# Decoder block on one Trainium2 core: a fourth step by seven products in every second early block, low parts in two halves, and changed service of banks and first transposes

## The chip, the cores and the metric

The kernel runs on one core of one Trainium2 chip. A core has a matrix engine (TensorE, PE in the profile; its weight loads are shown as PEld), VectorE (DVE), ScalarE (ACT), GpSimd (POOL) and SyncE (SP), each with an instruction queue of its own that is worked through in order, and DMA queues that SP, ACT and POOL feed. Matrix products are accumulated in eight banks of PSUM; everything else lives in SBUF or in DRAM. The metric is the device time of one execution in microseconds, as the median of the runs shown.

## The reference

One layer of a hybrid decoder on 256 tokens of 2048 channels, in float32. A normalised input is multiplied by one wide matrix; its columns feed dilated window attention and a gated linear recurrence, the two results are mixed by per-channel gates, and a SwiGLU feed-forward stage follows.

```python
a = rmsnorm(h, norm_mix_pre[layer])
proj = a @ w_in[layer]
q_a, k_a, v_a, q_r, f_r, i_r, g_r, gate_a, gate_r = split_columns(proj)
...
y = jax.nn.sigmoid(gate_a) * (attn @ w_attn_branch[layer]) + jax.nn.sigmoid(gate_r) * (r_out @ w_hgrn_branch[layer])
h = h + rmsnorm(y @ w_mix_out[layer], norm_mix_post[layer])
a = rmsnorm(h, norm_ffn_pre[layer])
gt, up = jnp.split(a @ w_ffn_gate_up[layer], [D_FF], axis=-1)
ff = (jax.nn.silu(gt) * up) @ w_ffn_down[layer]
h = h + rmsnorm(ff, norm_ffn_post[layer])
```

`g_r` passes through silu and a gain, the gates through a sigmoid; the values and `i_r` are only scaled by the row's norm factor.

## The kernel before

**Products in parts.** Each float32 operand is split into a high part (a ScalarE copy to a rounded type) and a low part (VectorE: operand minus high part). One product of a 128-row tile is then three TensorE instructions: high by high, high by low, low by high. The weights stream through SBUF: SP loads a tile `raw` (three buffers), `split` makes the parts two steps ahead of their use (`AHEAD` = 2), `multiply` or `multiply_wide` issues the products.

**Order.** The order is written out by hand. The loop at line 1346 takes step n of all blocks and issues, in this order: the block's `pre` if it is its first step; the split of step n+2 and the load behind it (lines 1350 to 1352); the products of step n; a piece of the evacuation that is under way (`advance(evacs)`); a piece of each lane (`advance_lanes`: lane 0 holds the opening's norm and tables, lane 1 the sums `pair_sums`). What stands earlier in this order stands earlier in each engine's queue. Evacuations are generators; each `yield` ends a piece.

**Blocks.** The run begins with two narrow blocks for the two halves of `g_r` (COL_GR), eight steps each of 12 products and 1024 weight columns in all. During the first of them `transpose_in` also brings x in, two 128-column pieces at a time: four transposes on TensorE, two copies on ScalarE (line 498), two low parts on VectorE (line 502). Their evacuation is `evac_g`. Then come eight wide blocks, the **early blocks**, 0 to 7: gates, values and `i`, 1024 columns each, eight steps each of 256 rows. Their evacuation `evac_kept` adds, scales and writes the result to DRAM (`kept`); it is read back later by GpSimd's queue. After them come the forget and query columns of the recurrence, the query and key columns with attention worked in between, the branches, the mix, ten wide feed-forward blocks and two wide down blocks.

**Steps by seven.** A wide step covers two row tiles, two column halves and two token halves: eight products, 24 instructions (a plain step). Where the order marks it, the step is done by seven products of sums (Strassen's scheme), 21 instructions. For that VectorE and ScalarE form, in `split_wide`: sums of weights (lines 333, 339, 340), their high parts (338, 341), the high part of the differences' operand `dh` (344), the low part of the sums (345) and the low part `dl` (347). The sums of x for it come from `pair_sums` and are kept in `x7`. Four products of each block (p1, p6, p5, p7) have banks of their own. After the block's last seven step, `gather` (lines 392 to 396) copies p1 and makes four sums; after the block's last step, `evac_kept` adds the other four banks to them. The two sets of four banks swap from block to block (`flip`). In the early and feed-forward blocks three steps of eight are by seven; the order is `EIGHT`: the pairs are (row pair, by seven), so steps 2, 4 and 6 are by seven.

**Buffers.** High parts `w` and low parts `wl` have three buffers, so the parts of step n+2 can be written once step n-1's products are done. `sum`, `dh` and `dl` have one buffer each. All 512-wide evacuation tiles `e` share six.

The lines to follow are 36 to 38 (orders), 319 to 348 (`split_wide`), 388 to 397 (`gather`), 619 to 620 (masks), 642 to 648 (transposes and sums), 663 to 677 (`evac_kept`), 738 to 754 (`evac_g`), 1293 to 1299 (early blocks) and 1346 to 1377 (the loop).

Of the kernel before, what the change touches and what calls it, by code (L numbers as in the profile page):

```python
# [13 lines left out]
F32 = mybir.dt.float32  # L14
# [5 lines left out]
P = 128  # L20
# [12 lines left out]
COL_QR, COL_FR, COL_IR, COL_GR = 9216, 10240, 11264, 12288  # L33
COL_GA, COL_GB = 13312, 15360

X7 = H7 = (0, 1, 2)
EIGHT = [(3, 0), (4, 0), (0, 1), (5, 0), (1, 1), (6, 0), (2, 1), (7, 0)]
DOWN = [[(m, m in by7) for m in range(KF // 2)] for by7 in (range(4, 20, 3), range(3, 19, 3))]

# [50 lines left out]
def tile_hybrid_block(ctx: ExitStack, tc: tile.TileContext, t, out):  # L90
# [105 lines left out]
        return pool["now"].tile([P, 512], F32, tag="p", bufs=n, name=nm(s))  # L196

    cs = kp.tile([P, 2, S], F32, name="cs")
    amask = kp.tile([P, 2, 512], F32, name="amask")
    lmask = kp.tile([P, len(LEVELS), 64], F32, name="lmask")  # L200
    gainr = kp.tile([P, HW], F32, name="gainr")
    tabs = kp.tile([P, 4, S], F32, name="tabs")
    bounds = kp.tile([P, 64], F32, name="bounds")
    lb, lb1 = bounds[:, :8], bounds[:, 8:16]


    blocks, seq, units = [], [], []
# [111 lines left out]
    def split_wide(st):  # L319

        b, raw = st.block, st.raw
        m, by7 = b.order[st.i]
        prep = b.prep(m, by7) if b.prep else iter(())
        next(prep, None)
        hi, lo = wslot(), p3("wl", F32R, 2048, 3)
        if not by7:
            nc.scalar.activation(hi, raw, AF.Copy)  # L327
            next(prep, None)
            nc.vector.tensor_sub(lo, raw, hi.bitcast(F32))  # L329
            st.parts = hi, lo  # L330
            return
        s, d = p3("sum", F32, 2048, 1), raw[:, 512:]
        nc.vector.tensor_sub(  # L333
            s[:, :1024].rearrange("p (a c) -> p a c", a=2),
            raw[:, 512:1536].rearrange("p (a c) -> p a c", a=2),
            raw[:, None, :512].to_broadcast([P, 2, 512]),
        )
        nc.scalar.activation(hi[:, :1024], s[:, :1024], AF.Copy)  # L338
        nc.vector.tensor_add(s[:, 1024:1536], raw[:, 512:1024], s[:, 512:1024])
        nc.vector.tensor_sub(s[:, 1536:], raw[:, 1536:], s[:, 1024:1536])  # L340
        nc.scalar.activation(hi[:, 1024:], s[:, 1024:], AF.Copy)  # L341
        next(prep, None)
        dhi, dlo = p3("dh", F32R, 1536, 1), p3("dl", F32R, 1536, 1)
        nc.scalar.activation(dhi, d, AF.Copy)  # L344
        nc.vector.tensor_sub(lo, s, hi.bitcast(F32))  # L345
        next(prep, None)
        nc.vector.tensor_sub(dlo, d, dhi.bitcast(F32))  # L347
        st.parts = hi, lo, dhi, dlo
# [230 lines left out]
    def opening():  # L579
        ss, s2 = small("ss"), small("s2")  # L580
        yield from sumsq(ss, xt[:3])
        nc.scalar.dma_start(gainr, t["hgrn_norm_gain"].to_broadcast([P, HW]))
        nc.scalar.dma_start(rowg[0:16], t["norm_ffn_pre"][0].rearrange("(a p) -> a p", p=P))
        nc.scalar.dma_start(
            rowg[16:32], t["hgrn_lower_bounds"].rearrange("l (a p) -> (l a) p", p=P)
        )
        nc.scalar.dma_start(cs, t["rope"])
        yield from sumsq(ss, xt[3:], 3)
        add_parts(s2[:, :2], ss)
        rsqrt_mean(r1c, s2[:, :2], D)  # L590
# [12 lines left out]
        nc.tensor.transpose(ps[:, :32], rowg[:32], ident[:32, :32])  # L603
        yield
        nc.vector.tensor_copy(colg[:, 16:48], ps[:, :32])
        l0, l1 = colg[:, 32:40], colg[:, 40:48]
        m, e0, e1 = small("m"), small("e0"), small("e1")
        nc.vector.tensor_max(m, l0, l1)
        nc.vector.tensor_sub(e0, l0, m)
        nc.vector.tensor_sub(e1, l1, m)  # L610
        nc.scalar.activation(e0, e0, AF.Exp)
        nc.scalar.activation(e1, e1, AF.Exp)
        nc.vector.tensor_add(e1, e0, e1)
        nc.vector.reciprocal(e1, e1)
        nc.vector.tensor_mul(lb, e0, e1)
        nc.vector.tensor_scalar(lb1, lb, -1.0, 1.0, op0=OP.mult, op1=OP.add)
        ready.add("lb")
        yield
        nc.sync.dma_start(amask, t["amask"])
        nc.sync.dma_start(lmask, t["lmask"])  # L620

    def keep_warm(n):

# [38 lines left out]

    def evac_kept(key, fn):
        def go(b):
            dst = keep(key, 1024)
            for s, g in ((0, 0), (0, 1), (1, 0), (1, 1)):
                src = b.bank[s, g]
                if b.rest:
                    e = b.rest[s, g]
                    nc.vector.tensor_add(e, src, e)  # L670
                    src = e
                else:
                    e = eslot()
                nc.scalar.activation(e, src, fn, scale=r1c[:, s : s + 1])
                nc.scalar.dma_start(dst[:, s, g * 512 : (g + 1) * 512], e)
            yield
        return go

    def end_early():
        flush(evacs)  # L680
        enter("middle")
        attnT.append(Split("attnT", 8))
        recT.append(Split("recT", 8))
        for half in range(2):
            gN[half] = hslot("g")
            back(gN[half], ("g", half), 0, 512, True)
            iN[half] = hslot("v")
            back(iN[half], "i", 512 * half, 512 * half + 512, True)

    def values_back(half):  # L690

# [46 lines left out]
    def evac_g(half):  # L738
        def go(banks):
            while "r1c" not in ready:  # L740
                yield
            dst, there = hslot("g"), keep(("g", half), 512)
            for i in range(2):
                ps = banks[i]
                s = ptile("sig")
                nc.scalar.activation(s, ps, AF.Sigmoid, scale=r1c[:, i : i + 1])
                yield
                nc.vector.scalar_tensor_tensor(  # L748
                    out=s, in0=ps, scalar=r1c[:, i : i + 1], in1=s, op0=OP.mult, op1=OP.mult
                )  # L750
                nc.vector.tensor_mul(dst[:, i, :], s, gainr[:, half * 512 : (half + 1) * 512])
                nc.gpsimd.dma_start(there[:, i, :], dst[:, i, :])
                yield
        return go
# [33 lines left out]
    def attention(pair, hh):  # L788
# [4 lines left out]
        for par in range(2):  # L793
            own = slice(par * P, (par + 1) * P)
            ps = aux()
            for g in range(3):
# [6 lines left out]
            p = ptile("p")  # L803
            m = small("m")
            nc.vector.tensor_tensor_reduce(
                out=p, in0=ps, in1=amask[:, par, :], scale=1.0, scalar=3e38,
                op0=OP.add, op1=OP.min, accum_out=m[:, 0:1],
            )
            nc.scalar.activation(p, p, AF.Exp, scale=-1.0, bias=m[:, 0:1], accum_out=m[:, 1:2])
# [27 lines left out]
    def recurrence(half):  # L837
# [36 lines left out]
        def products(lev, w):  # L874

            ps = aux()
            if w < 64:
                for e in range(8):
# [5 lines left out]
                yield  # L884
                nc.vector.copy_predicated(
                    at.rearrange("p (e n w) -> p e n w", e=8, w=2 * w)[:, :, :, w:],
                    lmask[:, lev, :].rearrange("p (n w) -> p n w", w=w)[:, None, :, :]
                    .to_broadcast([P, 8, 64 // w, w]).bitcast(I32),
                    ps.rearrange("p (e n w) -> p e n w", e=8, w=w),
                )  # L890
# [403 lines left out]
             (COL_GA + 1024, ("a", 1), AF.Sigmoid), (COL_GB + 1024, ("r", 1), AF.Sigmoid)]  # L1294
    early += [(COL_V + 1024 * g, ("v", g), AF.Copy) for g in range(3)] + [(COL_IR, "i", AF.Copy)]
    for n, (col, key, fn) in enumerate(early):
        add_seven(w_in, (col, col + 512), EIGHT, xT, lambda m: x7[m],
                  evac_kept(key, fn), flip=n % 2 == 1, turn=1,
                  pre=(lambda: flush(lanes[1])) if n == 0 else None)
    for half in range(2):  # L1300
        add_wide(w_in, KD, COL_FR + 512 * half, xT, evac_f(half))
        if half == 0:
# [27 lines left out]
    for j in range(2):  # L1330
        add_seven(t["w_ffn_down"][0], (1024 * j, 1024 * j + 512), DOWN[j], act,
                  lambda m: a7[m], evac_down, prep=prep_act, flip=j == 1,
                  pre=begin_down if j == 0 else None, turn=3 if j == 0 else None)

    load_x(0, 0, 256)
    load(0, 0)
    load_x(0, 256, 512)
# [8 lines left out]
    for n, st in enumerate(seq):  # L1346
        b, i = st.block, st.i
        if i == 0 and b.pre:
            b.pre()
        if n + AHEAD < len(seq):  # L1350
            split(seq[n + AHEAD])
            load_behind(seq[n + AHEAD])
        if n >= len(seq) - 3:
            continue
        if type(b) is Wide:
            multiply_wide(st)
            if i == b.last7:
                gather(b)
        else:
            multiply(st)  # L1360
            if b.post:
                b.post(i)
        advance(evacs)
        if turns and type(turns[0]) is not list:
            advance(turns)
        advance_lanes()
        if type(b) is not Wide:
            if st.last:
                evacs.append(b.evac(b.banks))
            continue  # L1370
        if i == b.turn:
            flush(evacs)
            if turns:
                turn_act(turns.popleft(), b)
        if st.last:
            evacs.append(b.evac(b))
            advance(evacs)
# [63 lines left out]
```

## Time and profile before

| | |
|---|---|
| runs | 1718.56, 1719.61, 1720.99 us |
| median | 1719.61 us |
| profiled execution, whole time | 1718.82 us |
| profiled execution, span from first to last instruction | 1717.0 us |
| granted TensorE clock | 0.999 |
| busy: TensorE, VectorE, ScalarE, GpSimd | 1700.6, 1373.6, 900.3, 21.7 us |
| eight early blocks | about 58 to 394 us |

A timeline row gives start in us, length in us, engine, line, operation, result and sources, sizes, and, in square brackets, how long the engine was idle before it and what ended the idle time. A row that stands for several instructions ends in their count. The lines of a group give count, busy time, mean length in ns and idle time before. Lengths of TensorE's instructions overlap (each is shown as some 0.39 us), so time on TensorE is best read from starts.

### The profile page before, as it was taken

The page shows a single profiled execution, that of the slowest core. Times are in us where ns is not written, and L with a number is a line of the kernel's source. Part 1 is how long each engine was busy: PE and PEld are TensorE (multiplying, and loading weights), DVE is VectorE, ACT ScalarE, POOL GpSimd, SP SyncE. Part 2 cuts the span into 40 slices and gives each one's busy share as a digit, 9 for nine tenths or more (in the row PEclk, how much of TensorE's full clock was granted, in tenths as well). Part 3 has the DMA queues.
Part 4 walks back from the last instruction along what each step waited for, and adds up shares of the span by engine and source line. Part 5 has one row for each costly group of instructions (what it writes and reads, how often), then busy time and mean ns, then how long its engine had stood idle before and what let it go on. Part 6 is the DMA issues. An engine that isn't in the chain of part 4 may idle for free.

```text
span 1717.0 us, 21554 instructions
## 1 busy us (share of the span) xinstructions
PE 1700.6 (99%) x8347; PEld 1428.2 (83%) x8347; DVE 1373.6 (80%) x1497; ACT 900.3 (52%) x1014; POOL 21.7 (1%) x38
## 2 busy tenths in 40 slices
PE   9999999999999999999999999999999999999997
PEld 6788888888888898888888878888888888888886
DVE  6888888885677887877666578888888888898998
ACT  6555555554435434544444466555555555665663
POOL 0000000000000000000000000000000000000000
PEclk9999999999999999999999999999999999999999
DMA  7666666667544645565456745555555555666653
GB/s 264 234 242 231 228 221 220 226 234 244 191 148 160 221 160 172 179 202 168 163 173 201 246 165 196 197 198 200 201 201 202 201 202 197 219 197 214 202 197 115
DMA packets 208741, 344.77 MB, mean 201 GB/s; under 512 B 10960, under 2 KB 77696, under 8 KB 208640
## 3 DMA queue, kind: packets, MB, share of 16 engines
q1 hardware_dynamic: 198496, 318.61, 55.0%
q10 hardware_dynamic: 7232, 14.31, 2.3%
q0 software_dynamic: 2912, 10.49, 1.8%
q8 instruction: 65, 1.06, 0.3%
q14 instruction: 36, 0.29, 0.0%
HBM read 331.83 MB, written 11.53 MB: 200 GB/s over the span
## 4 chain that ended last, share of the span: by engine, by line
PE 94%; DVE 3%; ACT 1%; DMA 1%; issue 1%; SPq 0%; ACTq 0%; DVEq 0%
PE acc L131 62%; PE aux L131 31%; DVE w L293 1%; DMA raw<-in_w_in 0%; PE aux L818 0%; DMA gpost<-in_norm_mix_post 0%; PE aux L491 0%; PE acc L1132 0%; DVE fz L1261 0%; PE aux L1132 0%; ACT w L327 0%; PE aux L479 0%; ACT junk L1215 0%; ACT w L292 0%; DVE sig L748 0%
## 5 line engine op out<-in xcount | busy, mean ns | idle before, releaser
L293 DVE TENSOR_TENSOR w<-raw,w 128x1024 fp32r<-128x1024 f32 (+1 forms) x225 | 274.2, 1219 | 189.4 <-ACT w L292 188.8
L292 ACT ACTIVATE w<-raw 128x1024 fp32r<-128x1024 f32 (+1 forms) x225 | 236.9, 1054 | 294.1 <-PE acc L131 248.3
L131 PE MATMUL acc<-xT,w 128*128 128x256 f32 (+1 forms) x2048 | 370.4, 339 | 0.0
L131 PEld LDWEIGHTS acc<-xT,w 128*128 128x128 f32 x2048 | 311.6, 188 | 43.3
L329 DVE TENSOR_TENSOR wl<-raw,w 128x2048 fp32r<-128x2048 f32 x122 | 279.0, 2286 | 41.6 <-ACT w L327 41.5
L327 ACT ACTIVATE w<-raw 128x2048 fp32r<-128x2048 f32 x122 | 232.9, 1909 | 110.1 <-PE aux L131 43.9
L345 DVE TENSOR_TENSOR wl<-sum,w 128x2048 fp32r<-128x2048 f32 x66 | 151.2, 2291 | 68.9 <-ACT w L341 68.8
L131 PE MATMUL acc<-w,hT 128*128 128x512 f32 x622 | 181.5, 391 | 0.3 <-ACT hT L498 0.3
L338 ACT ACTIVATE w<-sum 128x1024 fp32r<-128x1024 f32 x66 | 70.2, 1063 | 188.4 <-DVE sum L333 176.7
L131 PE MATMUL acc<-w,xT 128*128 128x512 f32 x536 | 155.8, 392 | 2.2 <-ACT xT L498 1.6
L131 PEld LDWEIGHTS acc<-w,hT 128*128 128x128 f32 x622 | 116.0, 188 | 24.7 <-ACT hT L498 0.5
L131 PE MATMUL aux<-w,hT 128*128 128x512 f32 x430 | 135.6, 389 | 0.0
L131 PEld LDWEIGHTS acc<-w,xT 128*128 128x128 f32 x536 | 99.7, 188 | 24.2 <-ACT xT L498 1.9
L347 DVE TENSOR_TENSOR dl<-raw,dh 128x1536 fp32r<-128x1536 f32 x66 | 115.6, 1751 | 0.0
L131 PE MATMUL aux<-w,xT 128*128 128x512 f32 x344 | 108.5, 389 | 0.0
L344 ACT ACTIVATE dh<-raw 128x1536 fp32r<-128x1536 f32 x66 | 97.3, 1474 | 0.0
L131 PEld LDWEIGHTS aux<-w,hT 128*128 128x128 f32 x430 | 80.7, 188 | 16.8
L131 PE MATMUL acc<-w,yT 128*128 128x512 f32 x384 | 88.2, 390 | 0.1
L131 PEld LDWEIGHTS acc<-w,yT 128*128 128x128 f32 x384 | 71.8, 188 | 15.3 <-DVE w L293 0.6
L131 PE MATMUL acc<-w,a 128*128 128x512 f32 x268 | 83.7, 389 | 0.0
L131 PE MATMUL aux<-wl,hT 128*128 128x512 f32 x215 | 83.6, 389 | 0.0
L131 PE MATMUL acc<-wl,hT 128*128 128x512 f32 x215 | 83.6, 389 | 0.0
(257 smaller groups left out, 2669.7 us busy)
## 6 DMA issues: line engine op xcount, KB each, us to landing
raw<-in_w_in SPq DMA_DIRECT2D x271, 512.0 KB, 4.6
raw<-in_w_ffn_gate_up SPq DMA_DIRECT2D x176, 512.0 KB, 4.4
raw<-in_w_ffn_down SPq DMA_DIRECT2D x88, 512.0 KB, 4.8
raw<-in_w_mix_out SPq DMA_DIRECT2D x32, 512.0 KB, 4.9
kept<-e ACTq DMA_DIRECT2D x32, 256.0 KB, 4.3
raw<-in_w_hgrn_branch SPq DMA_DIRECT2D x16, 512.0 KB, 4.5
raw<-in_w_attn_branch SPq DMA_DIRECT2D x16, 512.0 KB, 4.4
v<-kept POOLq DMA_DIRECT2D x8, 512.0 KB, 7.1
```

The lines of the kernel that those rows point to most:

```text
L131: nc.tensor.matmul(ps, lhsT, rhs, start=start, stop=stop, skip_group_check=True)
L292: nc.scalar.activation(wh[:, k], raw[:, k], AF.Copy)
L293: nc.vector.tensor_sub(wl[:, k], raw[:, k], wh[:, k].bitcast(F32))
L327: nc.scalar.activation(hi, raw, AF.Copy)
L329: nc.vector.tensor_sub(lo, raw, hi.bitcast(F32))
L338: nc.scalar.activation(hi[:, :1024], s[:, :1024], AF.Copy)
L344: nc.scalar.activation(dhi, d, AF.Copy)
L345: nc.vector.tensor_sub(lo, s, hi.bitcast(F32))
L347: nc.vector.tensor_sub(dlo, d, dhi.bitcast(F32))
```

## The change

- `X7` has four members, so a fourth pair of x's tiles gets its sums. A second order `FOUR` has steps 1, 3, 5 and 6 by seven; odd early blocks use it, even ones keep `EIGHT`.
- `dh` and `dl` have two buffers in the early stage.
- In early and feed-forward blocks the low part of the sums is made in two halves of 1024. In the down blocks (`b.prep`) it stays whole.
- The masks `amask` and `lmask` are allocated in the middle stage and loaded by GpSimd's queue at its beginning, no longer by SP's queue in the opening.
- `evac_kept` does its four bank additions first, then the four activations, two in each piece; the writes to DRAM go by GpSimd's queue, no longer by ScalarE's.
- `evac_g` reads the banks on ScalarE alone: a sigmoid and a scaled copy for each side, all in the first piece; VectorE multiplies afterwards, from SBUF.
- The second g block's first evacuation piece is issued at the start of early block 0, where lane 1 was flushed before; lane 1 is flushed at the start of block 1.
- In the first two steps of the run, the split of step n+2 and the load behind it are issued after the step's products and transposes.

```diff
-X7 = H7 = (0, 1, 2)
+X7, H7 = (0, 1, 2, 3), (0, 1, 2)
+FOUR = [(4, 0), (0, 1), (5, 0), (1, 1), (6, 0), (2, 1), (3, 1), (7, 0)]
 EIGHT = [(3, 0), (4, 0), (0, 1), (5, 0), (1, 1), (6, 0), (2, 1), (7, 0)]
...
-    amask = kp.tile([P, 2, 512], F32, name="amask")
-    lmask = kp.tile([P, len(LEVELS), 64], F32, name="lmask")
...
+    masks = {}
...
         next(prep, None)
-        dhi, dlo = p3("dh", F32R, 1536, 1), p3("dl", F32R, 1536, 1)
+        dhi, dlo = (p3(x, F32R, 1536, 2 if pool["name"] == "early" else 1) for x in ("dh", "dl"))
         nc.scalar.activation(dhi, d, AF.Copy)
-        nc.vector.tensor_sub(lo, s, hi.bitcast(F32))
+        for x in (slice(0, 2048),) if b.prep else (slice(0, 1024), slice(1024, 2048)):
+            nc.vector.tensor_sub(lo[:, x], s[:, x], hi[:, x].bitcast(F32))
         next(prep, None)
         nc.vector.tensor_sub(dlo, d, dhi.bitcast(F32))
...
-        yield
-        nc.sync.dma_start(amask, t["amask"])
-        nc.sync.dma_start(lmask, t["lmask"])
...
     def evac_kept(key, fn):
         def go(b):
-            dst = keep(key, 1024)
-            for s, g in ((0, 0), (0, 1), (1, 0), (1, 1)):
-                src = b.bank[s, g]
-                if b.rest:
-                    e = b.rest[s, g]
-                    nc.vector.tensor_add(e, src, e)
-                    src = e
-                else:
-                    e = eslot()
-                nc.scalar.activation(e, src, fn, scale=r1c[:, s : s + 1])
-                nc.scalar.dma_start(dst[:, s, g * 512 : (g + 1) * 512], e)
+            dst, at = keep(key, 1024), [(0, 0), (0, 1), (1, 0), (1, 1)]
+            for k in at:
+                nc.vector.tensor_add(b.rest[k], b.bank[k], b.rest[k])
+            for s, g in at:
+                e = b.rest[s, g]
+                nc.scalar.activation(e, e, fn, scale=r1c[:, s : s + 1])
+                nc.gpsimd.dma_start(dst[:, s, g * 512 : (g + 1) * 512], e)
+                if (s, g) == (0, 1):
+                    yield
             yield
...
             back(iN[half], "i", 512 * half, 512 * half + 512, True)
+        for key, shape in (("lmask", [P, len(LEVELS), 64]), ("amask", [P, 2, 512])):
+            masks[key] = pool["now"].tile(shape, F32, name=key)
+            nc.gpsimd.dma_start(masks[key], t[key])
...
             dst, there = hslot("g"), keep(("g", half), 512)
+            s = [ptile("sig") for _ in banks]
+            for i, ps in enumerate(banks):
+                nc.scalar.activation(s[i], ps, AF.Sigmoid, scale=r1c[:, i : i + 1])
+                nc.scalar.activation(dst[:, i, :], ps, AF.Copy, scale=r1c[:, i : i + 1])
+            yield
             for i in range(2):
-                ps = banks[i]
-                s = ptile("sig")
-                nc.scalar.activation(s, ps, AF.Sigmoid, scale=r1c[:, i : i + 1])
-                yield
-                nc.vector.scalar_tensor_tensor(
-                    out=s, in0=ps, scalar=r1c[:, i : i + 1], in1=s, op0=OP.mult, op1=OP.mult
-                )
-                nc.vector.tensor_mul(dst[:, i, :], s, gainr[:, half * 512 : (half + 1) * 512])
+                nc.vector.tensor_mul(dst[:, i, :], dst[:, i, :], s[i])
+                nc.vector.tensor_mul(
+                    dst[:, i, :], dst[:, i, :], gainr[:, half * 512 : (half + 1) * 512]
+                )
                 nc.gpsimd.dma_start(there[:, i, :], dst[:, i, :])
                 yield
...
-        add_seven(w_in, (col, col + 512), EIGHT, xT, lambda m: x7[m],
+        add_seven(w_in, (col, col + 512), FOUR if n % 2 else EIGHT, xT, lambda m: x7[m],
                   evac_kept(key, fn), flip=n % 2 == 1, turn=1,
-                  pre=(lambda: flush(lanes[1])) if n == 0 else None)
+                  pre=({0: lambda: advance(evacs), 1: lambda: flush(lanes[1])}).get(n))
...
+    def ahead(n):
+        if n + AHEAD < len(seq):
+            split(seq[n + AHEAD])
+            load_behind(seq[n + AHEAD])
+
...
         if i == 0 and b.pre:
             b.pre()
-        if n + AHEAD < len(seq):
-            split(seq[n + AHEAD])
-            load_behind(seq[n + AHEAD])
+        if n >= 2:
+            ahead(n)
...
             if b.post:
                 b.post(i)
+        if n < 2:
+            ahead(n)
         advance(evacs)
```

The uses of the masks in attention and recurrence read `masks["amask"]` and `masks["lmask"]`; nothing else in them changes.

More of the change, by code (lines that the diff above doesn't have):

```diff
@@ L805, in attention @@
             nc.vector.tensor_tensor_reduce(
-                out=p, in0=ps, in1=amask[:, par, :], scale=1.0, scalar=3e38,
+                out=p, in0=ps, in1=masks["amask"][:, par, :], scale=1.0, scalar=3e38,
                 op0=OP.add, op1=OP.min, accum_out=m[:, 0:1],
@@ L886, in products @@
                     at.rearrange("p (e n w) -> p e n w", e=8, w=2 * w)[:, :, :, w:],
-                    lmask[:, lev, :].rearrange("p (n w) -> p n w", w=w)[:, None, :, :]
+                    masks["lmask"][:, lev, :].rearrange("p (n w) -> p n w", w=w)[:, None, :, :]
                     .to_broadcast([P, 8, 64 // w, w]).bitcast(I32),
```

## The prediction

> **What bounds the kernel now.** I read the page's busy shares first, then the waits of TensorE, then the timeline of the first 140 us engine by engine, because every part of the change that can matter lies there.
>
> ```profile
> PE 1700.6 (99%) x8347; PEld 1428.2 (83%) x8347; DVE 1373.6 (80%) x1497; ACT 900.3 (52%) x1014; POOL 21.7 (1%) x38
> ...
> 62.00 0.39 PE L131 MATMUL aux<-wl,xT 128*128 128x512 f32 x1
> ...
> 68.80 0.39 PE L131 MATMUL aux<-wl,xT 128*128 128x512 f32 x1
> ```
>
> TensorE is never off the path. A busy share of 99% says little, as ends are modelled, so I take starts: the two rows are 30 products apart, 6.80 us, so one 512-wide product costs 0.227 us. A plain step (24 products) is 5.44 us, a step by seven products (21) 4.76 us. Each plain step turned into seven can save 0.68 us at most; the change turns one in each of blocks 1, 3, 5 and 7, **2.7 us in all**. The rest is waits of TensorE, and it has few:
>
> ```profile
> 71.79 0.39 PE L131 MATMUL acc<-w,so 128*128 128x512 f32 x1
> 73.52 0.50 PE L131 MATMUL acc<-w,so 128*128 128x512 f32 x1 [1.35 <-DVE sig L748]
> ...
> 74.10 0.39 PE L131 MATMUL acc<-w,so 128*128 128x512 f32 x1
> 74.91 0.50 PE L131 MATMUL acc<-w,so 128*128 128x512 f32 x1 [0.43 <-DVE sig L748]
> ...
> 81.85 0.39 PE L131 MATMUL aux<-dh,xT 128*128 128x512 f32 x1
> 83.32 0.50 PE L131 MATMUL aux<-dl,xT 128*128 128x512 f32 x1 [1.08 <-DVE dl L347]
> ```
>
> By starts, these lose 73.52-71.79-0.23 = 1.50, then 0.58 and 1.24 us, and each restart costs 0.1 more: **3.6 us in block 0**. The first two wait for banks that the g evacuation of the block before still holds, the third for the low part of the differences (dl).
>
> **Part 1: first transposes served sooner.**
>
> ```profile
> 9.98 1.23 DVE L293 TENSOR_TENSOR w<-raw,w 128x1024 fp32r<-128x1024 f32 x1 [1.61 <-ACT w L292]
> 10.83 0.60 PE L491 MATMUL aux<-ident,x 128*128 128x128 f32 x4
> ...
> 11.58 1.06 ACT L292 ACTIVATE w<-raw 128x1024 fp32r<-128x1024 f32 x1 [1.63 <-DMA raw<-in_w_in]
> 12.54 1.55 ACT L498 ACTIVATE xT<-aux,colg 128x256 fp32r<-128x256 f32 x4
> 13.05 0.73 PE L131 MATMUL acc<-w,xT 128*128 128x512 f32 x2 [1.62 <-ACT xT L498]
> 13.81 1.65 DVE L502 SCALAR_TENSOR_TENSOR xT<-aux,colg,xT 128x256 fp32r<-128x256 f32 x4
> ...
> 17.13 3.02 PE L131 MATMUL acc<-w,xT 128*128 128x512 f32 x12
> ```
>
> ScalarE holds the split of the first g block's step 2, which waits for its DMA until 11.58, ahead of the transposes' copies, though the second pair of transposes ended at 11.43. With the order turned, the four copies run from 9.97 to about 12.3, the four low parts on VectorE from 11.2 to 13.2, the split of step 2 from 12.3 (ScalarE) and 13.35 to 14.6 (VectorE). TensorE starts step 1 at 11.3 in place of 13.05 and without its second wait; 12 products and four transposes (2.7 + 0.6) bring step 2 to 14.7 in place of 17.13; its first low part, 14.6, is wanted at 14.95. **-2.4 us.** The splits of steps 2 and 3 come later relative to TensorE, with 0.2 to 0.4 us to spare; if that cover fails, up to 0.5 comes back. Step 3's load is no cover problem: SP's issues for step 8 wait for VectorE's split of step 3, 17.9 where it was 16.9, and step 8 is split some 11 us later.
>
> **Part 2: evac_g on ScalarE alone.** For each half of g, ScalarE now runs a sigmoid and a copy for both sides in one go.
>
> ```profile
> 41.38 0.69 ACT L746 ACTIVATE sig<-acc,r1c 128x512 f32<-128x512 f32 x1
> 41.97 1.05 ACT L292 ACTIVATE w<-raw 128x1024 fp32r<-128x1024 f32 x1
> ...
> 43.53 1.22 DVE L293 TENSOR_TENSOR w<-raw,w 128x1024 fp32r<-128x1024 f32 x1
> ...
> 54.47 0.69 DVE L419 TENSOR_TENSOR f<-xT 128x512 f32<-128x512 f32 x1
> ...
> 56.13 2.29 DVE L329 TENSOR_TENSOR wl<-raw,w 128x2048 fp32r<-128x2048 f32 x1
> 61.53 1.22 DVE L333 TENSOR_TENSOR sum<-raw 128x1024 f32<-128x1024 f32 x1
> ...
> 95.67 0.60 ACT L392 ACTIVATE e<-acc 128x512 f32<-128x512 f32 x1
> ```
>
> Half 0: three more ScalarE operations (0.60 + 0.68 + 0.60, less overlap) come ahead of the split at 41.97, which ends at 44.65, so VectorE's part starts at 44.7, not 43.53. VectorE has no slack from there to 58.42, when the row of 56.13 ends just as block 0's second product wants it (58.4). Its own work is 0.1 us shorter (two multiplications where a scalar_tensor_tensor and one stood). **+1.0 us**; were there 1 us of slack that I miss, 0.
>
> Half 1: the banks are free by 63, long before 72, so the 2.3 us of bank waits go. But VectorE is late next. Its queue from 61.53: the first seven step ends 0.8 sooner (below), 68.5; two multiplications, 1.33; the sums of the fourth pair, which X7 adds, 1.66 (54.47 to 56.13); a plain low part to 73.7; two multiplications, 75.0; the next seven step, dl at 81.9. TensorE, without the bank waits (1.50 + 0.58 + 0.2), reaches that step's first product at 81.85 - 2.28 = 79.57 and wants dl at 79.8: 2.1 late and 0.1 for the restart, where 3.6 was lost. **-1.4 us** (bounds: 0, if VectorE falls as far behind as it gains, to -3.6, if it keeps up). A delay in half 0 moves both by as much.
>
> **Part 3: a seven step on VectorE.** The low part of the sums in two halves:
>
> ```profile
> 110.19 2.29 DVE L345 TENSOR_TENSOR wl<-sum,w 128x2048 fp32r<-128x2048 f32 x1 [2.29 <-ACT w L341]
> ...
> 116.27 1.22 DVE L333 TENSOR_TENSOR sum<-raw 128x1024 f32<-128x1024 f32 x1
> ...
> 119.94 1.48 ACT L344 ACTIVATE dh<-raw 128x1536 fp32r<-128x1536 f32 x1
> 120.07 2.29 DVE L345 TENSOR_TENSOR wl<-sum,w 128x2048 fp32r<-128x2048 f32 x1 [1.13 <-ACT w L341]
> ...
> 122.28 1.75 DVE L347 TENSOR_TENSOR dl<-raw,dh 128x1536 fp32r<-128x1536 f32 x1
> 123.95 2.28 DVE L329 TENSOR_TENSOR wl<-raw,w 128x2048 fp32r<-128x2048 f32 x1
> ...
> L131 PE MATMUL aux<-w,hT 128*128 128x512 f32 x430 | 135.6, 389 | 0.0
> ```
>
> Now 7.68 us (116.27 to 123.95), 1.13 of it waiting for ScalarE. The first half (1.22) fills the wait, the second starts at 120.07 and ends at 121.29, dl starts when ScalarE ends dh, 121.46, and ends at 123.2: **6.86 us to the next start, 6.94 to the end of dl**. Bounds: 6.5 with no wait at all (1.25 for the first row, 0.7 and 0.6 for the two sums, 1.14 for each half, 1.67 for dl, start to start); 7.8 if the first half waits for the second high part after all. In the feed-forward blocks the same split meets no wait of TensorE (the last row, from the page's groups: 0.0 idle before hT's products), so it is worth nothing there; without VectorE's slack it would cost 2 x 1.22 - 2.29 = 0.15 for each of 30 steps.
>
> **Part 4: four steps by seven.** The queue of VectorE through an odd block, on block 1's clock of before:
>
> ```profile
> 93.68 1.92 ACT L327 ACTIVATE w<-raw 128x2048 fp32r<-128x2048 f32 x1 [1.34 <-PE aux L131]
> ...
> 97.84 0.68 DVE L393 TENSOR_TENSOR e<-acc,e 128x512 f32<-128x512 f32 x1
> ...
> 100.63 2.28 DVE L329 TENSOR_TENSOR wl<-raw,w 128x2048 fp32r<-128x2048 f32 x1
> ...
> 102.83 2.48 DVE L670 TENSOR_TENSOR e<-aux,e 128x512 f32<-128x512 f32 x4
> ...
> 103.55 0.72 ACT L674 ACTIVATE e<-e,r1c 128x512 f32<-128x512 f32 x1 [3.03 <-DVE e L670]
> ...
> 103.63 0.39 PE L131 MATMUL acc<-w,xT 128*128 128x512 f32 x1
> ```
>
> Gather takes 97.84 to 100.63. Then, where a plain low part stood, comes step 1 by seven: to 107.49. Only then the four bank additions of the last block (2.48, less 0.09 of overlap), to 109.88. ScalarE has two activations queued behind the first of them (108.2 to 109.6), and **behind those the high part of step 2**, 109.5 to 111.4. So VectorE stands idle for 1.5 us; step 2's low part runs to 113.64, step 3 by seven has its dl at 120.58. TensorE starts step 0 at 103.63, step 1 at 109.07, step 2 at 113.83, step 3 at 119.27 and wants dl at 119.50: **1.1 late**. It starts step 4 at 125.2, step 5 at 130.7 (dl 129.6, in time), step 6 at 135.4, wanting dl at 135.65; VectorE has done plain, seven and seven from 120.50 (2.20, from 100.63 to 102.83, + 6.86 + 6.94) at 136.50: **0.85 late**. With two restarts 2.1 us are lost for 0.68 saved, +1.45 a block, **+5.8 in four**. In even blocks the queue is plain, plain, seven; TensorE wants the first dl at 114.7 and it is there at 112.2, so nothing is lost. Second buffers for dh and dl are what lets steps 5 and 6 follow each other; p-banks are free at 108.2 to 109.9, the first wanted at 110.4.
>
> **Part 5: the rest.** 32 writes move from ScalarE's queue to GpSimd's, behind nothing that is waited for; the reads back queue behind them only after the early blocks. The masks leave SP's queue (two issues) for GpSimd's at the end of the early blocks; four blocks of forget and query columns lie between that and line 885, which reads them. No time; without that cover, a few us of landing.
>
> ```profile
> 46.05 1.22 DVE L293 TENSOR_TENSOR w<-raw,w 128x1024 fp32r<-128x1024 f32 x1
> 46.45 0.70 POOL L752 DMA_DIRECT2D kept<-g  x1 [44.92 <-DVE g L751]
> ```
>
> A GpSimd issue of 0.70 us ran inside a VectorE subtraction, which kept its 1.22 us.
>
> **Sum.** -2.4 + 1.0 - 1.4 + 5.8 = **+3.0 us**. The profiled execution took 1718.82, 0.8 below the median 1719.61; so 1721.8 on its scale, **1722.6** as a median. 3.4 us (0.2%) is what a measurement tells from no change, so this stands just inside.
>
> **Rivals.** (a) *VectorE is not late in odd blocks*: decided where its queue through such a block is shorter by 1.1 us up to step 3 and by 1.9 up to step 6, say because ScalarE's two activations don't delay step 2 and a seven step is a little quicker. For it: VectorE is busy for only 80%, and in the waits before the change it misses one dl. Against: the queue order, and the row at 110.19, where the same activations ahead of the high parts made a seven step wait 2.29 us, not 1.13. Time: -2.4 + 1.0 - 1.4 - 2.7 = -5.5, 1714.1. Chance 0.16.
>
> (b) *The first half still waits for the second high part*, so a seven step takes 7.8: four of them up to step 6 of an odd block add 0.96 each, +3.8 a block, +15 in all, 1737.8. For it: all that the rows show is a subtraction that needs both parts. Against: in the trace's records the two additions of line 236, over halves of one tile that ScalarE wrote one after the other, carry a wait each. Chance 0.05.
>
> (c) *The start's gain doesn't last*, block 1 being held by loads or by its own chain of small operations: +2.4, 1725.0. Against: of the splits from 8 to 60 us only two wait for a load, 3.0 us, both before 12 us (last row). Chance 0.13.
>
> ```profile
>   DMA raw<-in_w_in: 3.0, 2
> ```
>
> (d) *GpSimd's issues hold up VectorE*: four of 0.55 in each odd block's queue, +2.2 each, +8.8, 1731.4; even blocks have 2.5 us to spare. The rows of 46 us speak against it. Chance 0.04. By the Trainium skill, GPSIMD Engine Reference (Specifications), GpSimd shares its SBUF interface with VectorE and contends with instructions of two SBUF inputs, as these subtractions are; by that (d) would hold, and the trace does not agree.
>
> (e) *A seven step at the lower bound, 6.5*: lateness 0.4 and 0.1 in place of 1.1 and 0.85, so 0.0 a block, and block 0 gains 0.7 more: -2.4 + 1.0 - 2.1 = -3.5, 1716.1. Chance 0.10.
>
> **Chances.** The forecast has 0.52, about half of it under +3.4. Faster: (a) and the better part of (e)'s spread, 0.20. Same: the rest of (e) and half the forecast, 0.34. Slower: the other half, (b), (c), (d), 0.46. The range runs from (a) to past (c): 1714.5 to 1728, leaving out 0.17; the forecast's own is 1720 to 1726.
>
> **What will show it.** Step 2 should start near 14.7 us; block 0's second product should wait about 1 us for the row of L329; no wait for L748's banks; each odd block should show two waits for dl, at its steps 3 and 6, of 0.8 to 1.1 us, with VectorE idle before step 2's low part; even blocks none. Odd blocks without waits make the prediction wrong on the fast side, waits at step 1 or in even blocks on the slow side.

## The result, and the profile after

| | before | after |
|---|---|---|
| median | 1720.46 us (20 runs, 1718.56 to 1722.28) | 1722.41 us (20 runs, 1721.93 to 1724.24) |
| ratio after / before | | 1.0015, 95% interval 1.0008 to 1.0022 |
| profiled execution, whole time | 1718.82 us | 1722.40 us |
| its span | 1717.0 us | 1720.6 us |

The changed kernel is slower by 0.15% (0.08 to 0.22%), less than the 0.2% that the prediction called a difference. The two profiled executions lie 3.6 us apart, the lowest runs 3.4, the medians 1.95; the last number is smaller, it seems, because in a part of the executions, and in more of those of the kernel before, TensorE's clock falls to half for some 3 us behind waits, which adds about 1.5 us (last section).

Table of what TensorE waited for, in the profile after: engine, tile, line, releaser; then the total in us, the number of times and the longest. (In the changed kernel line 131 is 132, 347 is 348.)

```profile
PE acc L132 <- DVE dl L348: 6.7, 8, 0.9
PE aux L132 <- DVE dl L348: 1.3, 1, 1.3
...
PE aux L132 <- DVE wl L329: 0.9, 1, 0.9
...
PE aux L132 <- ACT dh L344: 0.5, 1, 0.5
PE aux L492 <- DMA x<-in_x: 0.4, 1, 0.4
```

The bank waits for L748 and the transposes' wait for ScalarE's copies are gone. Eight waits for `dl` have come, two for each of four odd blocks. The timeline of the same profile has them in place, and the marks behind them:

```profile
15.01 0.71 PE L132 MATMUL acc<-w,xT 128*128 128x512 f32 x2
...
40.92 0.70 ACT L745 ACTIVATE g<-acc,r1c 128x512 f32<-128x512 f32 x1
41.49 1.07 ACT L292 ACTIVATE w<-raw 128x1024 fp32r<-128x1024 f32 x1
42.60 1.23 DVE L293 TENSOR_TENSOR w<-raw,w 128x1024 fp32r<-128x1024 f32 x1 [1.17 <-ACT w L292]
...
56.10 0.39 PE L132 MATMUL aux<-w,xT 128*128 128x512 f32 x1
57.42 0.50 PE L132 MATMUL aux<-wl,xT 128*128 128x512 f32 x1 [0.93 <-DVE wl L329]
...
79.05 0.50 PE L132 MATMUL aux<-dh,xT 128*128 128x512 f32 x1 [0.47 <-ACT dh L344]
80.84 0.50 PE L132 MATMUL aux<-dl,xT 128*128 128x512 f32 x1 [1.29 <-DVE dl L348]
...
98.14 1.22 DVE L333 TENSOR_TENSOR sum<-raw 128x1024 f32<-128x1024 f32 x1
100.72 2.43 DVE L346 TENSOR_TENSOR wl<-sum,w 128x1024 fp32r<-128x1024 f32 x2
103.31 1.76 DVE L348 TENSOR_TENSOR dl<-raw,dh 128x1536 fp32r<-128x1536 f32 x1 [0.15 <-ACT dh L344]
104.99 2.48 DVE L665 TENSOR_TENSOR e<-aux,e 128x512 f32<-128x512 f32 x4
105.70 1.34 ACT L668 ACTIVATE e<-e,r1c 128x512 f32<-128x512 f32 x2 [2.43 <-DVE e L665]
106.95 1.90 ACT L327 ACTIVATE w<-raw 128x2048 fp32r<-128x2048 f32 x1
108.88 2.29 DVE L329 TENSOR_TENSOR wl<-raw,w 128x2048 fp32r<-128x2048 f32 x1 [1.42 <-ACT w L327]
109.75 0.54 POOL L669 DMA_DIRECT2D kept<-e  x1 [1.88 <-ACT e L668]
...
118.08 0.50 PE L132 MATMUL acc<-dl,xT 128*128 128x512 f32 x1 [0.91 <-DVE dl L348]
134.12 0.50 PE L132 MATMUL acc<-dl,xT 128*128 128x512 f32 x1 [0.79 <-DVE dl L348]
...
397.89 0.85 PE L132 MATMUL acc<-xT,w 128*128 128x512 f32 x4
```

The last row is the first product behind the early blocks. The same three places before were:

```profile
58.16 0.39 PE L131 MATMUL aux<-w,xT 128*128 128x512 f32 x1
58.47 0.50 PE L131 MATMUL aux<-wl,xT 128*128 128x512 f32 x1
...
393.99 0.85 PE L131 MATMUL acc<-xT,w 128*128 128x512 f32 x4
```

Follow the lead of the changed kernel along these starts. At block 0's first product it is 58.16 - 56.10 = 2.06 us ahead; at its second, 58.47 - 57.42 = 1.05, so 1.0 was lost to the new wait. At the wait for `dl` in block 0 it is 83.32 - 80.84 = 2.48 ahead, so 1.4 was won. At the end of the early blocks it is 397.89 - 393.99 = 3.90 behind, so the blocks between lost 6.4, or 1.6 for each odd one. Behind that no part of the change wins or loses more than some tenths: the distance is 3.6 at the end of the span.

The order of the queues is visible too. ScalarE does the high part of step 2 (106.95) only after two activations (105.70), these after VectorE's bank additions (104.99), and these after the first step by seven. VectorE stands idle for 1.42 us at 108.88, and `dl` is late twice.

### The profile page after: what moved, and what is told of

Read it like the earlier page. It is cut to its first block, busy times and chain, and to the rows that moved or that the text cites. A ratio compares the mean times of both kernels' runs of the same rounds, so it can differ in the third digit from the quotient of the medians.

```text
span 1720.6 us, 21632 instructions
## 1 busy us (share of the span) xinstructions
PE 1699.2 (99%) x8334; PEld 1425.1 (83%) x8335; DVE 1404.6 (82%) x1577; ACT 908.2 (53%) x1027; POOL 40.1 (2%) x72
## 4 chain that ended last, share of the span: by engine, by line
PE 77%; DVE 1%; ACT 1%; issue 1%; ACTq 0%; DVEq 0%
PE acc L132 52%; PE aux L132 23%; PE aux L818 0%; PE acc L1132 0%; DVE fz L1261 0%; PE aux L1132 0%; DVE dl L348 0%; PE aux L480 0%; PE aux L492 0%; ACT junk L1215 0%; ACT dh L344 0%; ACTq L1016 0%; DVE e L1211 0%; DVE sum L333 0%; ACT w L292 0%
## 5 line engine op out<-in xcount | busy, mean ns | idle before, releaser
L329 DVE TENSOR_TENSOR wl<-raw,w 128x2048 fp32r<-128x2048 f32 x118 | 269.9, 2289 | 76.1 <-ACT w L327 74.9
L327 ACT ACTIVATE w<-raw 128x2048 fp32r<-128x2048 f32 x118 | 225.0, 1909 | 112.0 <-PE aux L132 49.6
L338 ACT ACTIVATE w<-sum 128x1024 fp32r<-128x1024 f32 x70 | 74.4, 1063 | 190.2 <-DVE sum L333 181.1
L346 DVE TENSOR_TENSOR wl<-sum,w 128x1024 fp32r<-128x1024 f32 (+1 forms) x128 | 168.6, 1321 | 0.0
L132 PE MATMUL acc<-w,xT 128*128 128x512 f32 x480 | 139.3, 393 | 0.3 <-DVE w L293 0.2
L348 DVE TENSOR_TENSOR dl<-raw,dh 128x1536 fp32r<-128x1536 f32 x70 | 123.0, 1757 | 8.8 <-ACT dh L344 6.7
L132 PEld LDWEIGHTS acc<-w,xT 128*128 128x128 f32 x480 | 89.2, 188 | 20.0 <-DVE w L293 1.6
L344 ACT ACTIVATE dh<-raw 128x1536 fp32r<-128x1536 f32 x70 | 103.1, 1473 | 0.0
L341 ACT ACTIVATE w<-sum 128x1024 fp32r<-128x1024 f32 x70 | 74.4, 1062 | 21.5 <-DVE sum L340 21.5
L333 DVE TENSOR_TENSOR sum<-raw 128x1024 f32<-128x1024 f32 x70 | 85.2, 1217 | 0.2 <-DMA raw<-in_w_ffn_down 0.2
L132 PE MATMUL aux<-w,a 128*128 128x512 f32 x268 | 83.7, 389 | 0.0
```

The source lines that it names most:

```text
L132: nc.tensor.matmul(ps, lhsT, rhs, start=start, stop=stop, skip_group_check=True)
L333: nc.vector.tensor_sub(s[:, :1024].rearrange("p (a c) -> p a c", a=2), raw[:, 512:1536].rearrange("p (a c) -> p a c", a=2), raw[:, None, : ...
L346: nc.vector.tensor_sub(lo[:, x], s[:, x], hi[:, x].bitcast(F32))
```

## Experiments

All are edits of the changed kernel (1722.41), except where another base is named; ratios are to the kernel before.

**Three of eight everywhere.**

```diff
-        add_seven(w_in, (col, col + 512), FOUR if n % 2 else EIGHT, xT, lambda m: x7[m],
+        add_seven(w_in, (col, col + 512), EIGHT, xT, lambda m: x7[m],
```

> The changed kernel with the order EIGHT in all early blocks; everything else of the change stays, the fourth pair's sums too. Order theory: no wait of TensorE for dl in odd blocks; each odd block loses its two waits (1.07 + 0.95 + 0.2 us) and pays 0.68 for three more products: 4 x -1.55 = -6.2 us against the changed kernel, so 1716.2 beside 1722.4, some 4.2 us under the kernel before. Rival, the waits have another source in the odd blocks (GpSimd's issues, the banks): the waits stay and the lost saving is added, +2.7 us, 1725.

Measured 1715.87 us, ratio 0.9972 (0.9962 to 0.9983). The eight waits are gone from the table of waits; the two of block 0 and that at 57 us stay. The fourth step by seven costs 6.5 us as it stands; the rest of the change is a gain of 4.6.

**The activations later.** All four activations of `evac_kept` go into the piece after the bank additions, behind step 2's high part.

```diff
                 nc.vector.tensor_add(b.rest[k], b.bank[k], b.rest[k])
+            yield
             for s, g in at:
...
-                if (s, g) == (0, 1):
-                    yield
             yield
```

> The changed kernel with the four activations of evac_kept one piece later: the bank additions in the piece at the end of the block, all four activations and writes in the piece after step 0's products, so behind the split of step 2. Order theory: step 2's high part starts 1.3 us sooner, VectorE's idle 1.4 us before its low part goes, the wait for dl at step 3 of odd blocks is gone and the one at step 6 is about 0.55 + 0.1: 4 x -1.5 = -6 us, 1716.3, the same time as with three of eight but with another trace. Rival, VectorE has too much work in an odd block wherever the activations stand: both waits stay near 1 us and the time is within 1 us of the changed kernel's.

Measured 1715.88, ratio 0.9976 (0.9967 to 0.9986). Its table of waits:

```profile
PE acc L132 <- DVE dl L348: 1.9, 4, 0.5
```

Eight waits have become four, all at step 6 (the first at 132.13). VectorE's low part of step 2 starts at 106.89, behind the bank additions without a pause:

```profile
104.50 2.48 DVE L665 TENSOR_TENSOR e<-aux,e 128x512 f32<-128x512 f32 x4
105.22 2.57 ACT L669 ACTIVATE e<-e,r1c 128x512 f32<-128x512 f32 x4 [0.62 <-DVE e L665]
...
106.89 2.28 DVE L329 TENSOR_TENSOR wl<-raw,w 128x2048 fp32r<-128x2048 f32 x1
```

What is left, 0.5 and a restart, is what the fourth step by seven saves, so this equals three of eight.

**All four activations first**, the opposite: the yield after the second activation is taken out.

> The suspected cost doubled: all four activations of evac_kept stand in the first piece, ahead of the high part of step 2. Order theory: 1.27 us more of ScalarE (two of 0.72 less overlap) ahead of step 2's high part in odd blocks, so a new wait of about 0.9 for step 2's low part and 1.3 at step 3's dl in place of 1.07, in all +1.2 us for each odd block, +5 us, 1727.3; even blocks have 2.5 us to spare and show no wait. Rival (VectorE's load or GpSimd's issues): no more than 0.5 us in all.

Measured 1728.24, ratio 1.0042 (1.0030 to 1.0055). The profiled execution took 1729.05, of which 1.7 us are a stretch of half clock in block 0 (last section); without it, it meets the forecast. VectorE's idle time before step 2's low part grows to 2.65 us, and the odd blocks have a third wait, four times in all:

```profile
PE acc L132 <- DVE dl L348: 7.5, 8, 1.1
PE acc L132 <- DVE wl L329: 2.8, 4, 0.7
```

**First g half as before.** In `evac_g`, half 0 gets back a sigmoid on ScalarE, then a scalar_tensor_tensor and a multiplication on VectorE, one side a piece.

> The changed kernel with evac_g of the first half as it was before (one sigmoid a piece, VectorE reads the banks); the second half as changed. Theory: the split behind the sigmoid is not held up, VectorE's chain up to early block 0 is 1 us sooner, and the wait of 1.1 us at block 0's second product is gone or under 0.2; -0.9 us, 1721.5. Rival: that wait comes from the earlier start (loads or the chain of small operations do not follow it), then it stays and the time is as the changed kernel's.

Measured 1721.08, ratio 1.0004 (0.9996 to 1.0013). The wait of 0.93 us at 57 us is gone from the table; VectorE's low part of block 0's first step starts at 53.44 instead of 55.09. The rest stays. So the three ScalarE operations ahead of one split do cost 1.0 to 1.3 us fifteen microseconds later.

**Start as before.**

```diff
-        if n >= 2:
-            ahead(n)
+        ahead(n)
...
-        if n < 2:
-            ahead(n)
```

> The first two steps of the run again issue the split of step n+2 ahead of their products; all else as changed. Theory (the order of the first transposes' copies is the whole gain of the start, and it lasts, since the chain of starts behind it moves as a block): step 2 of the first g block starts 2.1 us later, near 17.1, and all later marks with it; 1722.4 + 2.1 = 1724.5. Rival (the gain is taken back by the late splits further on, so that undoing it costs nothing): step 2 late, but the marks of block 1 unchanged, 1722.4.

Measured 1726.27, ratio 1.0030 (1.0018 to 1.0041): 3.9 more than the changed kernel, not 2.1. Its lowest run is 1724.32, 2.4 above the lowest of the changed kernel. The profile of this run shows where more was lost:

```profile
13.15 0.73 PE L132 MATMUL acc<-w,xT 128*128 128x512 f32 x2 [1.70 <-ACT xT L499]
14.44 3.94 PE L132 MATMUL acc<-w,xT 128*128 128x512 f32 x10 [0.56 <-DVE xT L503]
18.22 0.60 PE L492 MATMUL aux<-ident,x 128*128 128x128 f32 x4
18.58 0.71 PE L132 MATMUL acc<-w,xT 128*128 128x512 f32 x2
```

Ten products took 18.22 - 14.44 = 3.78 us; in the profile before the same ten took 2.44 (14.34 to the transposes at 16.78). TensorE's own pace had fallen, which none of the theories had: the granted clock is 0.50 from 14 to 16 us. The same comes again in block 0 of this profile (0.50 from 86 to 88 us). Of the 5.0 us between this profiled execution and that of the changed kernel, the slower products make up 1.9 us here and 1.6 there.

**Low part whole.**

```diff
-        for x in (slice(0, 2048),) if b.prep else (slice(0, 1024), slice(1024, 2048)):
+        for x in (slice(0, 2048),):
```

> The low part of the sums is made whole again in the early and feed-forward blocks; the fourth step by seven stays. Theory (VectorE's queue is what the odd blocks wait for, and a half fills the wait for the second high part): a step by seven takes some 7.7 us on VectorE in place of 6.85, and TensorE's waits grow by what piles up: step 3's by 2 x 0.8, step 6's by about as much again, so some 3.3 us for each of four odd blocks and 1 in block 0, about 14 in all: 1736.5. Rival (the halves are hidden behind the wait for ScalarE's part of the differences): under 1 us, 1722 to 1723.5.

Measured 1739.30, ratio 1.0108 (1.0094 to 1.0122). The rival falls. VectorE waits for the second high part again, and the waits for `dl` double. In the profiled execution, which took 1740.66, the clock is at half behind these waits in three stretches, and the products there start 0.2 us later each: 2.7 us in all from 82 us on, 1.6 from 142 and 1.6 from 214. The third stretch costs nothing, because the next wait for `dl` is shorter by as much (0.67 us, where it is 2.11 in block 1). The other two make up the 4.2 us above the forecast:

```profile
106.12 2.29 DVE L346 TENSOR_TENSOR wl<-sum,w 128x2048 fp32r<-128x2048 f32 x1 [1.12 <-ACT w L341]
...
110.00 2.47 DVE L665 TENSOR_TENSOR e<-aux,e 128x512 f32<-128x512 f32 x4
...
123.92 0.50 PE L132 MATMUL acc<-dl,xT 128*128 128x512 f32 x1 [1.94 <-DVE dl L348]
141.46 0.50 PE L132 MATMUL acc<-dl,xT 128*128 128x512 f32 x1 [2.11 <-DVE dl L348]
...
213.22 0.50 PE L132 MATMUL acc<-dl,xT 128*128 128x512 f32 x1 [1.93 <-DVE dl L348]
```

The step by seven takes 110.00 - 102.33 = 7.67 us on VectorE (its first sum starts at 102.33); with halves it was 104.99 - 98.14 = 6.85. So in the kernel with four steps by seven, where VectorE sets the end, the halves are worth more than any other part of the change. What they are worth with three, no run shows.

**Writes on ScalarE's queue** in `evac_kept`, in place of GpSimd's.

```diff
-                nc.gpsimd.dma_start(dst[:, s, g * 512 : (g + 1) * 512], e)
+                nc.scalar.dma_start(dst[:, s, g * 512 : (g + 1) * 512], e)
```

> The early blocks' writes go by ScalarE's queue again; all else as changed. Theory (ScalarE's queue between a block's bank additions and step 2's high part decides how late VectorE is): two issues stand ahead of that high part, some 0.45 us each, so step 3's wait grows by 0.9 to 1.0 in each odd block: 1726. Rival (GpSimd's issues hold VectorE up beside its subtractions): faster than the changed kernel, by up to 1 us for each odd block, 1718 to 1721.

Measured 1727.93, ratio 1.0041 (1.0027 to 1.0055); its profiled execution took 1726.63, 4.2 more than that of the changed kernel. Two issues and the pauses around them push the split to 108.02 and VectorE's low part to 109.97:

```profile
105.66 0.72 ACT L668 ACTIVATE e<-e,r1c 128x512 f32<-128x512 f32 x1 [2.43 <-DVE e L665]
106.41 0.35 ACTq L669 DMA_DIRECT2D kept<-e  x1
106.81 0.72 ACT L668 ACTIVATE e<-e,r1c 128x512 f32<-128x512 f32 x1 [0.43 <-DVE e L665]
107.57 0.33 ACTq L669 DMA_DIRECT2D kept<-e  x1
108.02 1.92 ACT L327 ACTIVATE w<-raw 128x2048 fp32r<-128x2048 f32 x1 [0.48 <-ACT e L668]
...
109.97 2.29 DVE L329 TENSOR_TENSOR wl<-raw,w 128x2048 fp32r<-128x2048 f32 x1 [2.56 <-ACT w L327]
```

The added delay shows at another place than was expected: step 3's longest wait grows only from 0.9 to 1.1 us, and a new wait of 0.6 us stands at step 2's low part in each odd block, as with all four activations first. Taking the issues from GpSimd gains nothing on balance. Since the run loads ScalarE by the same edit, it can't show alone that they don't hold VectorE up; the rows can. In the profile after, two issues (0.54 us at 109.75 and 0.55 at 110.49) run inside the low part that starts at 108.88, and it takes 2.29 us, as it does here without them.

**The good parts alone.** Three of eight, `X7` with three members (the fourth pair gets no sums), first g half as before; all else as changed.

> Every early block has three steps by seven, the fourth pair of x's tiles gets no sums, and the first g half is evacuated as before; the new start, the second g half's evacuation, the halves, the second buffers of dh and dl and the bank additions' order stay. Theory, from the marks of the run with three of eight (1715.9): the wait at 57 us goes (-1.0), and in block 0 VectorE is 1.66 us of sums less late for its first step by seven, where 2.2 us were lost (-1.7): 1713.3, some 7 under the kernel before. Rival (the fourth pair's sums lie in VectorE's slack, so that leaving them out gives nothing): 1715.

Measured 1712.74, ratio 0.9953 (0.9941 to 0.9966), 8.2 us under the 1720.98 measured beside it for the kernel before, so it beats both. All that is left of TensorE's waits in the early blocks:

```profile
PE aux L132 <- DVE dl L348: 0.4, 1, 0.4
```

**The same with the old start**, to see what the start is worth where nothing else waits for long.

> The version with three of eight and the first g half as before, with the start undone as well. Its only long waits of TensorE are then the two at the start (some 1.7 and 0.6 us lost between 13 and 15 us) and one of 0.6 us near 80 us. Theory (the start's order is worth 2.1 us; and two waits that make up some 2.2 us within 3.4 us let the granted clock fall to half for one such stretch in a part of the executions): the lowest run 1712.5 + 2.1 = 1714.6, and a spread of its runs of 1.5 us or more above that, where the version with the new start spreads over 1.2 us; in a profile that has the dip, the granted clock is near 0.5 between 14 and 18 us and 1.0 from 70 to 92 us. Rival (the dips come from elsewhere, or only with the waits of block 0): all runs within 1.2 us, 1714.5 to 1715.7.

Measured 1716.75 (11 runs, 1714.96 to 1718.77), ratio 0.9979 (0.9970 to 0.9987): 2.6 above the former from lowest run to lowest, 4.0 from median to median. Its runs spread over 3.8 us, those of the former over 1.2. Windows of TensorE in its profile (window, busy time in all, busy time of TensorE, granted clock, share of DMA, GB/s):

```profile
14.00:16.00 2.00, 1.44 (x4) 0.51 1.05 387
16.00:18.00 2.00, 2.00 (x7) 0.63 1.05 386
...
81.00:83.00 2.00, 1.61 (x7) 1.00 0.18 9
```

While TensorE works, the clock falls to half behind the start's two waits and nowhere else, so the rival falls. The products there lose 1.4 us, which doesn't account for the whole spread of 3.8; the rest is open.

**The good parts with four of eight.** `FOUR` again in odd blocks; the fourth pair's sums are made from block 0's fifth step on.

```diff
+        if n == 20:
+            lanes[1].append(pair_sums(xT, (3,), x7, lambda: rslot("so")))
```

> The same version with the fourth step by seven put back into odd blocks; the sums of the fourth pair of x's tiles are made from the fifth step of block 0 on, not before its first step by seven. Theory (each odd block gives up 1.55 us, 2 to 2.2 lost in two waits for 0.68 saved, whatever else the kernel does, and waits of 1 us alone don't make the clock fall): 1712.7 + 4 x 1.55 = 1718.9, waits for the low part of the differences at steps 3 and 6 of each odd block, spread within 1.2 us; some 1.5 more if the late sums push block 1. Rival (part of the loss in odd blocks came from the delay that VectorE brought with it from the g evacuation): 1713 to 1716.

Measured 1721.14 (11 runs, 1720.50 to 1721.42), ratio 1.0005 (0.9996 to 1.0014): 8.4 above the good parts alone, where 6.2 and perhaps 1.5 were expected. The late sums did push block 1:

```profile
PE acc L132 <- DVE dl L348: 6.9, 8, 1.1
...
PE acc L132 <- DVE wl L329: 1.0, 1, 1.0
```

The rival falls: the waits for `dl` are as long as in the changed kernel, though block 0 hands on no delay from the g evacuation. The clock doesn't fall in its profile, and its runs lie within 0.9 us: waits of 1 us some 7 to 16 us apart don't bring it.

## Why the prediction was right

**Sum.** +3.0 was forecast from one profiled execution to the other, 1721.8; it is +3.6, 1722.40, with the clock full in both. The median of 1722.41 meets the forecast of 1722.6 more closely, but partly by luck: the median shown for before was of three runs, that of twenty is 0.85 higher. By marks the start came out 0.3 worse than forecast and the four odd blocks 0.6 worse (6.4 for 5.8); the rest of the difference is some tenths behind the early blocks.

**Part 1**, -2.4 forecast, -2.1 in this profile. Step 1 starts at 11.33 (11.3 forecast), step 2 at 15.01 (14.7). In this execution the transposes waited 0.4 us for x's load; in the good parts alone, with the same start, step 2 starts at 14.65. The order is the whole gain, and it lasts: rival (c) falls with the two runs that undo it (+2.4 and +2.6 from lowest run to lowest). The prediction had no term for the clock, which the old start's waits can let fall.

**Part 2, half 0**, +1.0: measured 1.0, at the place and by the row named. **Half 1**, -1.4: measured -1.4. The wait moved from banks to `dl`, as written; its lateness was put at 2.1 at one place. It is there at two, 0.47 us of waiting for ScalarE's `dh`, which the prediction didn't name, and 1.29 for `dl`; by starts 2.2 us are lost.

**Part 3.** A step by seven of 6.86 us was forecast, 6.85 is measured; rival (b) was a step of 7.8 and (e) one of 6.5, and both are out. What (b)'s price would be, the run with the whole low part shows: +16.9 between the medians, some 14 between the profiled executions without the clock's share, where (b) had +15.

**Part 4**, +1.45 a block: 1.6 by marks. Two waits, at steps 3 and 6, of 0.91 and 0.79 us, for which 1.1 and 0.85 of lateness were forecast; none in even blocks. The cause, two activations ahead of step 2's high part, is shown by moving them each way: -6.5 and +5.8. They make the whole wait at step 3 and 0.3 us of that at step 6; the 0.5 left at step 6 stays without them, so they aren't its cause. Rival (a) was the case in which they don't delay step 2; its time was 1714.1, and 1715.88 is what is measured with them out of the way, with step 6 still waiting.

**Part 5.** No cost was forecast for the writes on GpSimd's queue, and rival (d) had 8.8 us for them; putting them back costs time. By the Trainium skill, GPSIMD Engine Reference (Specifications), GpSimd and VectorE contend for an SBUF interface; that these issues cost VectorE anything, no run here shows, and the low part at 108.88, beside two of them, kept its 2.29 us. The masks landed by 418 us and are first read at 472; nothing waits for them.

Not tried by themselves were the second half of `evac_g`, the second buffers of `dh` and `dl`, the order of the bank additions, and the fourth pair's sums; what is said of the second half of `evac_g` rests on the marks alone.

## What to carry to other kernels

A step by seven saves TensorE 0.68 us and asks VectorE for 6.85 - 2.21 = 4.6 more. In an odd block VectorE would have 4 x 6.85 + 4 x 2.21 + 2.4 (bank additions) + 2.8 (gather) = 41.4 us of work. TensorE has 4 x 4.76 + 4 x 5.44 = 40.8 then, and 41.5 with three steps by seven. So by this sum a fourth has next to nothing to win inside such a block, which agrees with the run with the activations later. An order in which VectorE brings a lead from the even block, where it has less work (36.8 us), was not tried. Add up the second engine's queue for the block before giving it work to relieve the first. And what decides a wait is often a small operation ahead of a split in another engine's queue: two activations of 0.7 us cost 6.5 us over the kernel. Where a change has several parts, try each without the others; here a gain of 8 us lay under a loss.

## What the runs showed of the hardware

TensorE's clock can fall to half for some 3 us after waits that are short; such a stretch is called a dip below. In the profile of three of eight, TensorE's windows behind the two waits of block 0 are

```profile
81.00:83.00 2.00, 2.00 (x7) 0.61 0.54 114
83.00:85.00 2.00, 2.00 (x7) 0.53 1.05 391
```

and in that of the changed kernel, with the same two waits,

```profile
81.00:83.00 2.00, 2.00 (x9) 1.00 0.47 120
83.00:85.00 2.00, 2.00 (x10) 1.00 1.06 391
```

From 85 us on the clock is 1.00 in both. The same waits let the clock fall in one execution and not in another. Of the profiles of the experiments, those of three of eight, all four activations first, first g half as before, start as before and low part whole have such a dip in block 0; the two with the old start have one at 14 us. Ahead of each of these lie two waits of TensorE within 4 us, by which over 2 us are lost. Two waits aren't needed: low part whole has two more dips, each behind one wait (2.11 us at 141.46, and 1.93 at 213.22), while the wait of 1.94 at 123.92 brought none. In the good parts alone and the same with four of eight, TensorE behind its first 10 us has no wait over 1.1 us; no profile of theirs has a dip, and the runs spread over 1.2 and 0.9 us. By the Trainium skill, TensorE: Matmul & The Clock Gate (Part 1), the array's clock is halved or full, by how busy it was in free-running windows of about 3.4 us; half clock for some 3 us (eight products of the run with three of eight start 0.2 us later each, 1.6 in all) and in some executions only agrees with that. Its table names an idle window as the condition; here waits of some 2 us in all were enough, with products between them or without.

For the result this means: 12 of the changed kernel's 20 runs lie between 1721.93 and 1722.48 and 8 between 1723.52 and 1724.24, with none between. The mean granted clock of each of the 12 is 0.998 or 0.999, that of each of the 8 is 0.997; 3.3 us at half clock would take 0.001 off the mean over 1720 us. The runs of before spread over 3.7 us, and the median is 1.6 above the profiled execution, where that of after is equal to it. Of the 54 runs of before that were measured beside the experiments, the 11 with a clock of 0.999 took 1719.59 us or less, the 16 with 0.997 or less took 1720.52 or more. So the longer runs of both kernels have the lower clock. Where in the execution it falls, and behind which wait, is an inference for these runs, as no profile of one was taken. The price of waits that add up to some 2 us within a few us is then more than their length: 1.4 to 2.7 us for each dip in the profiles here, times the share of executions in which the clock falls, and less where a later wait shrinks by it.
